# Four tiles for the modulation rows, four fetches ahead, in a two-layer hybrid block

## The chip, the cores and the metric

One core of one Trainium2 chip runs the kernel. The metric is the device time of one execution in microseconds (us); the time before is the median of three runs. The engines are called by their short names: PE (TensorE, matrix products; PEld is its weight load), DVE (VectorE), ACT (ScalarE), POOL (GpSimd) and SP (SyncE, which issues most transfers). DMA engines move data between memory and the core's own SBUF; PSUM takes the products.

## The reference

Two layers, 256 tokens of `x` and 256 of a context `ctx`, width 2048, float32. Each layer begins with a modulation: a vector of 2048 numbers times a matrix of 2048 x 6144, which gives a shift, a scale and a gate. The first layer (even) is a gated delta rule in two directions over 16 heads together with a short convolution; the second (odd) mixes within chunks and pools over rows.

```python
for layer in range(2):
    mod_x = silu(c) @ ada_w[layer] + ada_b[layer]      # 2048 -> 3 * 2048
    sh_x, sc_x, gt_x = split(mod_x, 3)
    h_x = rmsnorm(x, norm_w[layer]) * (1 + sc_x) + sh_x
    # the context likewise, in the first layer only
    if layer == 0:
        y_x, y_c = even_mixer(h_x, h_c, ...)           # delta rule, short convolution, projection out
    else:
        y_x = odd_stream(h_x @ o_w_in, ...)            # chunk mixing, pooling, projection out
    x = x + gt_x * y_x
return rmsnorm(x, final_norm_w)
```

The delta rule needs, per head, direction and chunk of 64 tokens, the inverse of a unit lower triangular matrix, and then a recurrence from chunk to chunk with a state S of 128 x 128.

## The kernel before

**Weights.** All large products run in float32 as three products of a high part H and a remainder L. `wchunk` (L195) fetches a chunk of 128 x 1024 numbers (512 KB) into a tile `raw` (four of them), ACT casts it to H, and DVE or POOL forms L = raw - H; H and L have four tiles each. PE then works through the chunk. The order of the code is not the order of the queues: a planner takes the program and puts each instruction on its engine's queue as soon as, by its own reckoning, the operands and the tile are there, earlier lines first. A transfer that needs a tile stays behind the last reader of the tile's previous content. On the chip every queue then runs strictly in its planned order.

**Stages.** First a projection of the first 1536 key columns with the modulation of the first layer's shift and scale (PE line L449; `h_cols` makes the normalized input and holds a tile `hf` of the modulation rows' pool), then keys and values (`wkv`, PE line L229, with `finish` and the decay rows `ab_rows`), some 180 to 560 us. Then four groups of four heads, some 560 to 1450 us: query and gate projections, the triangular inversion (tiles `Dg`, `LB`, `DT`, and `PTs`, `PTq` in the same places), the recurrence (`St`, `oacc`, `zk`) and the short convolution's projections (`wbb`); inversion and recurrence have high priority. Then the output projection (`wout0`, `projT`, PE lines L238 to L240), the second layer's normalized input `h1`, and from 1600 us on the second layer's projections.

**Modulation rows.** The remaining modulation (the gate of the first layer, all three parts of the second) is not a PE product: 256 steps each fetch a block of 128 x 512 numbers (256 KB) into a tile `araw` (L268) and DVE adds it, times one column of silu(c), to an accumulator `acc` (L274, L276). 16 steps make a segment; `acc` has two tiles. `ada_fin` (L278) sums a segment over the partitions on PE (`adc`), turns it by a second product and adds it to `modc`; the gates go through memory (`rowd`). `ada_step` (L298) is one step in program order: fetch of row u, accumulate of row u - 1, and the end of a segment some steps later. `wchunk` calls it at a rate per chunk, by stage 2.5, 0.6, 1.2 and 0.4; in the third stage no step is taken past the end of the second layer's shift and scale, and ahead of h1 the steps up to there are completed. `araw` has two tiles, in which the constant `mn` and every `hf` also pass.

**What stands beside it.** The first projection has its own tiles `k0`, `k0l` (two each) for H and L. In `ab_rows` the seven decay rows `w` to `br` are tiles of their own.

Of the kernel before, what the change touches and what calls it, by code (L numbers as in the profile page):

```python
# [9 lines left out]
F32 = mybir.dt.float32  # L10
# [7 lines left out]
P = 128  # L18
D = 2048
KT = 16  # L20
# [7 lines left out]
FCUT = (0, 3, 7, 12, 16)  # L28
TAIL = (5, 6)
HP = 1  # L30
FINK = 2
RATE = (2.5, 0.6, 1.2, 0.4)
LP = (0.5, 0.5, 0.4, 0.2)
# [88 lines left out]
def body(ctx: ExitStack, tc: tile.TileContext, T, dbg=None):  # L122
# [21 lines left out]
    whp = pool("wh", NB[1])  # L144
    wlp = pool("wl", NB[2])
# [46 lines left out]
    tick = [0.0, 0.0, 0, 0.0]  # L192

    def wchunk(src, nk, rp=None, hp=None, lp=None, sz=1024, HL=None):
        if extra[0] and hp is None:  # L195
            extra[1] += 1
            rp, hp, lp = extra[0][extra[1] % len(extra[0])]
        raw = (rp or wrawp).tile([P, sz], F32, name="raw", tag="raw")
        dma(raw, src)
        H = HL[0] if HL else (hp or whp).tile([P, sz], F32R, name="H", tag="H")  # L200
        S.copy(H, raw)  # L201
        L = HL[1] if HL else (lp or wlp).tile([P, sz], F32R, name="L", tag="L")
        tick[3] += LP[tick[2]]
        if tick[3] >= 1.0:
            tick[3] -= 1.0
            G.tensor_tensor(L, raw, H, ALU.subtract)  # L206
        else:
            V.tensor_tensor(L, raw, H, ALU.subtract)  # L208
        tick[1] += tick[0]
        while tick[1] >= 1.0:  # L210
            tick[1] -= 1.0
            if tick[2] != 2 or ada_n[0] <= 12 * KT + FINK:
                ada_step()
        return [t.rearrange("p (k c) -> p k c", k=nk) for t in (H, L)]

# [48 lines left out]
    def ada_load(u):  # L264
        w, col = segs[u // 64][:2]
        k, col = u % KT, col + u // KT % 4 * 512
        araw[u] = adap.tile([P, 512], F32, name="araw", tag="araw", bufs=2)
        dma(araw[u], w[k * P:(k + 1) * P, col:col + 512])  # L268

    def ada_acc(u):  # L270
# [22 lines left out]
            S.copy(r, t[0:KT])  # L293
            dma(rowd[gate].rearrange("(a b) -> a b", a=KT), r)

    ADA_N = 256 + 1 + FINK

    def ada_step(n=1):  # L298
        for _ in range(max(0, min(n, ADA_N - ada_n[0]))):
            u = ada_n[0]  # L300
            if u < 256:
                ada_load(u)
            if 1 <= u <= 256:
                ada_acc(u - 1)
            f = u - KT - FINK
            if f >= 0 and f % KT == 0:
                ada_fin(f // KT)
            ada_n[0] += 1
# [55 lines left out]
    with ExitStack() as ph1:  # L364
# [5 lines left out]
        with ExitStack() as ph0:  # L370
# [2 lines left out]
            cs32 = tp.tile([P, KT, 32], F32, name="cs32")  # L373
            V.memset(cs32, 0.0)
            S.copy(cs32[:, :, 0:2], cs)
            k0r, k0p, k0l = pool("k0r", 3, stack=ph0), pool("k0", 2, stack=ph0), pool("k0l", 2, stack=ph0)
            acc = [accp.tile([P, 2, 512], F32, name="kacc", tag=f"kacc{b}") for b in range(6)]

            def ada_cols(j):
# [20 lines left out]
            def load_consts():  # L400
                dma(cst, T["consts"][:, 0:578])
                S.copy(identr, ident)
                t = adap.tile([P, 512], F32, name="mn", tag="araw", bufs=2)[:, 0:256]
                dma(t, T["consts"][:, 578:834])
                S.copy(mneg, t.rearrange("p (a b) -> p a b", a=2))
                S.copy(selr, cst[:, 512:576])
# [22 lines left out]
            def h_cols(j, srcs=(0, 1)):  # L429
                tr = gp.tile([P, 4, P], F32, name="trp", tag="g")  # L430
                for s in srcs:
                    aH, aL = ((hxH, hxL), (hcH, hcL))[s]
                    for n in (2 * s, 2 * s + 1):
                        PE.transpose(tr[:, n, :], toks[n][:, j * P:(j + 1) * P], ident)
                    hf = adap.tile([P, 512], F32, name="hf", tag="araw", bufs=2)[:, 0:256]
                    S.activation(hf, tr[:, 2 * s:2 * s + 2, :].rearrange("p a b -> p (a b)"), AF.Identity,
                                 scale=mods[:, 1, j, s:s + 1], bias=mods[:, 0, j, s:s + 1])
                    split(aH[:, j, :], aL[:, j, :], hf)

            def k_load(e, j):  # L440
                return [t[:, 0] for t in wchunk(T["wset"][e, j], 1, rp=k0r, hp=k0p, lp=k0l, sz=768)]

            def k_part(w, j, ps, first, last, srcs):
                for n in range(6):
# [45 lines left out]
        def row(name):  # L490
            return ap.tile([64, 512], F32, name=name)
# [18 lines left out]
        def ab_rows():  # L510
# [47 lines left out]
                def v4(t):  # L558
                    return t.rearrange("p (c s k) -> p c s k", c=4, s=2)

                w, ng, xr, er, kr, lr, br = (row(n) for n in ("w_", "ng", "xr", "er", "kr", "lr", "br"))
                V.tensor_scalar(ng, gc, -1.0, None, ALU.mult)
                V.tensor_tensor(w.rearrange("p (s k) -> p s k", s=8), glf.unsqueeze(2).to_broadcast([64, 8, 64]),
                                gc.rearrange("p (s k) -> p s k", s=8), ALU.subtract)
# [106 lines left out]
    with ExitStack() as ph2:  # L671
# [6 lines left out]
        for grp in range(4):  # L678
# [48 lines left out]
            with (tc.high_priority() if HP else ExitStack()):  # L727
# [119 lines left out]
                if grp == 0:  # L847
                    tap("U", U.rearrange("p d c h i -> p (d c h i)"))

                St = A.tile([P, 2, 4, P], F32, name="St", tag="St")  # L850
                oacc = [A.tile([P, 4, P], F32, name=f"oacc{c}", tag=f"oacc{c}") for c in range(2)]
                seen = set()
                for s in range(4):
                    for d in range(2):
# [24 lines left out]
                            rh = r[:, h, :] if s > 0 else Vn[:, h, ch, :]  # L879
                            PE.matmul(z[:, h, :], U[:, d, ch, h, :], rh, start=True, stop=True)  # L880
                        if s < 3:
                            zk = A.tile([P, 4, P], F32, name="zk", tag=f"zk{d}")
                            for h in range(4):
                                S.activation(zk[:, h, :], z[:, h, :], AF.Copy, scale=nzs[:, d, ch, h0 + h:h0 + h + 1])
                        if ch < 2:
# [99 lines left out]
    with ExitStack() as ph3:  # L985
# [11 lines left out]
        out_proj(T["wout0"], yact, 0, x1, Wo, pss, (yb_part, [6, 7]), TAIL[0], post0, slots)  # L997
        extra[0] = []
        y_stack.close()
        ada_step(12 * KT + FINK + 1 - ada_n[0])  # L1000
        V.tensor_scalar(A1, mod1[:, KT:2 * KT], 1.0, None, ALU.add)
        V.tensor_tensor(A1, A1, normw[:, KT:2 * KT], ALU.mult)

# [188 lines left out]
```

## Time and profile before

| what | us |
|---|---|
| median of three runs | 2283.49 (2281.34 to 2284.37) |
| the profiled execution's own time | 2281.2 |
| its span | 2279.4 |
| PE busy | 2102.5 (92%) |
| DVE busy | 1511.8 (66%) |
| ACT busy | 992.0 (44%) |
| POOL busy | 547.9 (24%) |
| mean granted clock of PE | 0.968 |

The profile is of one execution. Durations are in us unless marked ns. A wait is the time for which an engine stood idle just before an instruction, put down to what came last; idle time of an engine costs something only where PE comes to stand for it. The granted clock is the share of PE's full clock of 2.4 GHz in a stretch; 0.5 is the lower level of 1.2 GHz.

### The profile page before, as it was taken

How to read it: one execution, taken by the hardware profiler on the slowest of the kernel's cores; microseconds unless marked ns; L12 is line 12 of the kernel's file. 1: busy time of each engine (PE TensorE's matmuls, PEld its weight loads, DVE VectorE, ACT ScalarE, POOL GpSimd, SP SyncE). 2: the span in 40 equal slices, each digit the busy share in tenths (PEclk: the TensorE clock that was granted, in tenths of full speed). 3: DMA queues.
4: the chain of work that ended last, by engine and by line, in shares of the span. 5: the costliest groups of instructions: out<-in, count | busy, mean ns of one | idle time of the engine just before them, and what ended most of it. 6: DMA issues, size and time to landing. Idle time of an engine off the chain costs nothing. (4 is left out here: it accounts for less than half of the span.)

```text
span 2279.4 us, 42114 instructions
## 1 busy us (share of the span) xinstructions
PE 2102.5 (92%) x17034; PEld 1951.4 (86%) x17034; DVE 1511.8 (66%) x2500; ACT 992.0 (44%) x1726; POOL 547.9 (24%) x258
## 2 busy tenths in 40 slices
PE   6998999899989988998899879898999999999998
PEld 4888989898979987998899868686789999999886
DVE  4336997658965896599658964666667676555445
ACT  4332354225544635553545354334444444444443
POOL 0112112123322332323232323232112111111221
PEclk9999999999989999999899989999999999999999
DMA  8776546668435663566356645686767656666664
GB/s 324 278 258 209 153 146 201 192 188 275 141 108 169 213 219 122 170 204 214 120 163 214 205 141 175 200 289 193 251 203 215 180 185 199 188 193 216 192 191 137
DMA packets 151267, 446.41 MB, mean 196 GB/s; under 512 B 16512, under 2 KB 23456, under 8 KB 150048
## 3 DMA queue, kind: packets, MB, share of 16 engines
q1 hardware_dynamic: 145936, 425.37, 58.7%
q0 software_dynamic: 5136, 18.35, 2.6%
q8 instruction: 133, 2.18, 0.4%
q14 instruction: 62, 0.51, 0.1%
HBM read 423.19 MB, written 20.46 MB: 195 GB/s over the span
## 5 line engine op out<-in xcount | busy, mean ns | idle before, releaser
L206 POOL TENSOR_TENSOR L<-raw,H 128x1024 fp32r<-128x1024 f32 (+1 forms) x205 | 508.7, 2483 | 1557.9 <-ACT H L201 1500.2
L201 ACT CAST H<-raw 128x1024 fp32r<-128x1024 f32 (+1 forms) x554 | 571.9, 1039 | 698.7 <-PE pj L229 302.3
L208 DVE TENSOR_TENSOR L<-raw,H 128x1024 fp32r<-128x1024 f32 (+1 forms) x349 | 447.8, 1285 | 311.2 <-ACT H L201 310.1
L229 PE MATMUL pj<-hxH,L 128*128 128x256 f32 x1856 | 537.7, 290 | 43.9 <-DVE L L208 43.7
L229 PE MATMUL pj<-hxH,H 128*128 128x256 f32 x1856 | 536.1, 289 | 4.8 <-DVE kacc L482 4.8
L229 PE MATMUL pj<-hxL,H 128*128 128x256 f32 x1856 | 535.0, 288 | 0.0
L229 PEld LDWEIGHTS pj<-hxH,L 128*128 128x128 f32 x1856 | 360.2, 194 | 51.6 <-DVE L L208 48.1
L229 PEld LDWEIGHTS pj<-hxH,H 128*128 128x128 f32 x1856 | 360.2, 194 | 6.9 <-DVE kacc L482 5.0
L229 PEld LDWEIGHTS pj<-hxL,H 128*128 128x128 f32 x1856 | 360.3, 194 | 1.4 <-issue 0.4
L276 DVE SCALAR_TENSOR_TENSOR acc<-araw,cs,acc 128x512 f32<-128x512 f32 x240 | 244.9, 1020 | 134.3 <-DMA araw<-in_ada 84.0
L229 PE MATMUL pj<-h1H,H 128*128 128x256 f32 x1024 | 290.6, 284 | 0.8 <-DVE yo L1052 0.8
L229 PE MATMUL pj<-h1H,L 128*128 128x256 f32 x1024 | 289.8, 283 | 0.0
L229 PE MATMUL pj<-h1L,H 128*128 128x256 f32 x1024 | 289.8, 283 | 0.0
L229 PEld LDWEIGHTS pj<-h1H,H 128*128 128x128 f32 x1024 | 196.5, 192 | 1.1 <-PE adc L286 0.8
L229 PEld LDWEIGHTS pj<-h1L,H 128*128 128x128 f32 x1024 | 196.5, 192 | 0.0
L229 PEld LDWEIGHTS pj<-h1H,L 128*128 128x128 f32 x1024 | 196.5, 192 | 0.0
L229 PE MATMUL pj<-hcH,H 128*128 128x256 f32 x320 | 92.0, 287 | 0.0
L229 PE MATMUL pj<-hcH,L 128*128 128x256 f32 x320 | 91.6, 286 | 0.0
L229 PE MATMUL pj<-hcL,H 128*128 128x256 f32 x320 | 91.5, 286 | 0.0
L238 PE MATMUL pj<-H,y1H 128*128 128x512 f32 x192 | 76.0, 396 | 0.0
L240 PE MATMUL pj<-H,y1L 128*128 128x512 f32 x192 | 75.9, 396 | 0.0
L239 PE MATMUL pj<-L,y1H 128*128 128x512 f32 x192 | 75.9, 395 | 0.0
(433 smaller groups left out, 3852.3 us busy)
## 6 DMA issues: line engine op xcount, KB each, us to landing
raw<-in_wbb SPq DMA_DIRECT2D x128, 512.0 KB, 4.1
raw<-in_wout SPq DMA_DIRECT2D x128, 512.0 KB, 4.5
araw<-in_ada SPq DMA_DIRECT2D x192, 256.0 KB, 3.4
raw<-in_ada SPq DMA_DIRECT2D x64, 512.0 KB, 6.4
raw<-in_wpz SPq DMA_DIRECT2D x64, 512.0 KB, 4.1
raw<-in_wuz SPq DMA_DIRECT2D x64, 512.0 KB, 3.9
raw<-in_wkv SPq DMA_DIRECT2D x40, 512.0 KB, 4.7
araw<-in_ada0g SPq DMA_DIRECT2D x64, 256.0 KB, 3.6
```

Of the source, the lines that this page charges most:

```text
L201: S.copy(H, raw)
L206: G.tensor_tensor(L, raw, H, ALU.subtract)
L208: V.tensor_tensor(L, raw, H, ALU.subtract)
L229: PE.matmul(o[:, e * 256:(e + 1) * 256] if m > 1 else o, w, a[t][:, k, :], start=st and i == 0 and e == 0, stop=sp and i == 2, skip_group_ ...
L238: PE.matmul(o, xH[:, t], H[:, kk, :], start=st, stop=False, skip_group_check=True)
L239: PE.matmul(o, xH[:, t], L[:, kk, :], start=False, stop=False, skip_group_check=True)
L240: PE.matmul(o, xL[:, t], H[:, kk, :], start=False, stop=sp, skip_group_check=True)
L276: V.scalar_tensor_tensor(aacc[u // KT], raw, cs[:, k, 0:1], aacc[u // KT], ALU.mult, ALU.add)
```

## The change

`araw` gets four tiles, and a row's accumulate stands four steps behind its fetch instead of one. The number of steps grows from 259 to 262, the end of a segment comes three steps later, and the two guards that count steps grow alike. Three further things change: the first projection uses the common H and L tiles (four each) instead of its own; two rows of `ab_rows` reuse the tiles of `y` and `q`; and `St`, `oacc` (both chunks in one tile) and `zk` (both directions in one tile) of the recurrence pass through the tiles `LB`, `DT` and `Dg` of the inversion.

```diff
--- before.py
+++ after.py
@@ -28,6 +28,7 @@
 FCUT = (0, 3, 7, 12, 16)
 TAIL = (5, 6)
 HP = 1
+LA = 4
 FINK = 2
 RATE = (2.5, 0.6, 1.2, 0.4)
 LP = (0.5, 0.5, 0.4, 0.2)
@@ -209,7 +210,7 @@
         tick[1] += tick[0]
         while tick[1] >= 1.0:
             tick[1] -= 1.0
-            if tick[2] != 2 or ada_n[0] <= 12 * KT + FINK:
+            if tick[2] != 2 or ada_n[0] < 12 * KT + FINK + LA:
                 ada_step()
         return [t.rearrange("p (k c) -> p k c", k=nk) for t in (H, L)]
 
@@ -264,7 +265,7 @@
     def ada_load(u):
         w, col = segs[u // 64][:2]
         k, col = u % KT, col + u // KT % 4 * 512
-        araw[u] = adap.tile([P, 512], F32, name="araw", tag="araw", bufs=2)
+        araw[u] = adap.tile([P, 512], F32, name="araw", tag="araw", bufs=LA)
         dma(araw[u], w[k * P:(k + 1) * P, col:col + 512])
 
     def ada_acc(u):
@@ -293,16 +294,16 @@
             S.copy(r, t[0:KT])
             dma(rowd[gate].rearrange("(a b) -> a b", a=KT), r)
 
-    ADA_N = 256 + 1 + FINK
+    ADA_N = 256 + LA + FINK
 
     def ada_step(n=1):
         for _ in range(max(0, min(n, ADA_N - ada_n[0]))):
             u = ada_n[0]
             if u < 256:
                 ada_load(u)
-            if 1 <= u <= 256:
-                ada_acc(u - 1)
-            f = u - KT - FINK
+            if LA <= u < 256 + LA:
+                ada_acc(u - LA)
+            f = u - KT - FINK - LA + 1
             if f >= 0 and f % KT == 0:
                 ada_fin(f // KT)
             ada_n[0] += 1
@@ -373,7 +374,7 @@
             cs32 = tp.tile([P, KT, 32], F32, name="cs32")
             V.memset(cs32, 0.0)
             S.copy(cs32[:, :, 0:2], cs)
-            k0r, k0p, k0l = pool("k0r", 3, stack=ph0), pool("k0", 2, stack=ph0), pool("k0l", 2, stack=ph0)
+            k0r = pool("k0r", 3, stack=ph0)
             acc = [accp.tile([P, 2, 512], F32, name="kacc", tag=f"kacc{b}") for b in range(6)]
 
             def ada_cols(j):
@@ -400,7 +401,7 @@
             def load_consts():
                 dma(cst, T["consts"][:, 0:578])
                 S.copy(identr, ident)
-                t = adap.tile([P, 512], F32, name="mn", tag="araw", bufs=2)[:, 0:256]
+                t = adap.tile([P, 512], F32, name="mn", tag="araw", bufs=LA)[:, 0:256]
                 dma(t, T["consts"][:, 578:834])
                 S.copy(mneg, t.rearrange("p (a b) -> p a b", a=2))
                 S.copy(selr, cst[:, 512:576])
@@ -432,13 +433,13 @@
                     aH, aL = ((hxH, hxL), (hcH, hcL))[s]
                     for n in (2 * s, 2 * s + 1):
                         PE.transpose(tr[:, n, :], toks[n][:, j * P:(j + 1) * P], ident)
-                    hf = adap.tile([P, 512], F32, name="hf", tag="araw", bufs=2)[:, 0:256]
+                    hf = adap.tile([P, 512], F32, name="hf", tag="araw", bufs=LA)[:, 0:256]
                     S.activation(hf, tr[:, 2 * s:2 * s + 2, :].rearrange("p a b -> p (a b)"), AF.Identity,
                                  scale=mods[:, 1, j, s:s + 1], bias=mods[:, 0, j, s:s + 1])
                     split(aH[:, j, :], aL[:, j, :], hf)
 
             def k_load(e, j):
-                return [t[:, 0] for t in wchunk(T["wset"][e, j], 1, rp=k0r, hp=k0p, lp=k0l, sz=768)]
+                return [t[:, 0] for t in wchunk(T["wset"][e, j], 1, rp=k0r, hp=whp, lp=wlp, sz=768)]
 
             def k_part(w, j, ps, first, last, srcs):
                 for n in range(6):
@@ -558,7 +559,7 @@
                 def v4(t):
                     return t.rearrange("p (c s k) -> p c s k", c=4, s=2)
 
-                w, ng, xr, er, kr, lr, br = (row(n) for n in ("w_", "ng", "xr", "er", "kr", "lr", "br"))
+                w, ng, xr, er, kr, lr, br = (row(n) for n in ("w_", "ng", "xr", "er", "kr", "y_", "q_"))
                 V.tensor_scalar(ng, gc, -1.0, None, ALU.mult)
                 V.tensor_tensor(w.rearrange("p (s k) -> p s k", s=8), glf.unsqueeze(2).to_broadcast([64, 8, 64]),
                                 gc.rearrange("p (s k) -> p s k", s=8), ALU.subtract)
@@ -847,8 +848,10 @@
                 if grp == 0:
                     tap("U", U.rearrange("p d c h i -> p (d c h i)"))
 
-                St = A.tile([P, 2, 4, P], F32, name="St", tag="St")
-                oacc = [A.tile([P, 4, P], F32, name=f"oacc{c}", tag=f"oacc{c}") for c in range(2)]
+                St = I.tile([P, 2, 4, P], F32, name="St", tag="LB")
+                oac2 = I.tile([P, 2, 4, P], F32, name="oacc", tag="DT")
+                oacc = [oac2[:, c] for c in range(2)]
+                zk2 = I.tile([P, 2, 4, P], F32, name="zk", tag="Dg")
                 seen = set()
                 for s in range(4):
                     for d in range(2):
@@ -879,7 +882,7 @@
                             rh = r[:, h, :] if s > 0 else Vn[:, h, ch, :]
                             PE.matmul(z[:, h, :], U[:, d, ch, h, :], rh, start=True, stop=True)
                         if s < 3:
-                            zk = A.tile([P, 4, P], F32, name="zk", tag=f"zk{d}")
+                            zk = zk2[:, d]
                             for h in range(4):
                                 S.activation(zk[:, h, :], z[:, h, :], AF.Copy, scale=nzs[:, d, ch, h0 + h:h0 + h + 1])
                         if ch < 2:
@@ -997,7 +1000,7 @@
         out_proj(T["wout0"], yact, 0, x1, Wo, pss, (yb_part, [6, 7]), TAIL[0], post0, slots)
         extra[0] = []
         y_stack.close()
-        ada_step(12 * KT + FINK + 1 - ada_n[0])
+        ada_step(12 * KT + FINK + LA - ada_n[0])
         V.tensor_scalar(A1, mod1[:, KT:2 * KT], 1.0, None, ALU.add)
         V.tensor_tensor(A1, A1, normw[:, KT:2 * KT], ALU.mult)
```

## Rows read from the trace of the kernel before

**Rows 1.** The page's first part: the span, and busy time, share and number of instructions of each engine.

```profile
span 2279.4 us, 42114 instructions
PE 2102.5 (92%) x17034; PEld 1951.4 (86%) x17034; DVE 1511.8 (66%) x2500; ACT 992.0 (44%) x1726; POOL 547.9 (24%) x258
```

**Rows 2.** The view of waits for PE alone (who waited, for whom: us in total, times, longest us), in four stretches one after the other: 182 to 560 us (three rows), 570 to 1310 us (one), 570 to 660 us (one), 1456 to 1674 us (four).

```profile
PE kvp L598 <- DVE kvT L362: 20.8, 10, 4.6
PE pj L229 <- DVE kacc L482: 4.8, 1, 4.8
PE adr L291 <- DVE modc L288: 1.8, 1, 1.8
...
PE pj L229 <- DVE L L208: 43.7, 20, 7.4
...
PE pj L229 <- DVE L L208: 11.3, 5, 5.9
...
PE pj L239 <- DVE L L208: 10.1, 6, 4.4
PE pg L239 <- DVE L L208: 3.2, 2, 2.2
PE pg L238 <- ACT H L201: 2.9, 1, 2.9
...
PE pj L240 <- DVE h1L L345: 1.5, 1, 1.5
```

**Rows 3.** The page's fifth part, groups of instructions: line, engine, operation, out<-in, shape, count | busy us, mean ns of one | idle time of the engine before them, and what ended most of it.

```profile
L206 POOL TENSOR_TENSOR L<-raw,H 128x1024 fp32r<-128x1024 f32 (+1 forms) x205 | 508.7, 2483 | 1557.9 <-ACT H L201 1500.2
L201 ACT CAST H<-raw 128x1024 fp32r<-128x1024 f32 (+1 forms) x554 | 571.9, 1039 | 698.7 <-PE pj L229 302.3
...
L276 DVE SCALAR_TENSOR_TENSOR acc<-araw,cs,acc 128x512 f32<-128x512 f32 x240 | 244.9, 1020 | 134.3 <-DMA araw<-in_ada 84.0 <-DMA araw<-in_ada0g 48.6
```

**Rows 4.** The view of the tile araw, its last line: time from a fetch's issue to its landing, least, median and most, of the whole run and then of the stretch from 505 to 545 us.

```profile
DMA to landing us min/median/max: 2.5/3.5/7.8
...
DMA to landing us min/median/max: 2.9/5.3/7.8
```

**Rows 5.** The view of waits for DVE alone, its rows on the modulation rows, in three stretches: 182 to 560 us (two rows), 570 to 1310 us, 1456 to 1674 us.

```profile
DVE acc L276 <- DMA araw<-in_ada0g: 48.6, 31, 3.3
DVE acc L276 <- DMA araw<-in_ada: 20.7, 16, 3.0
...
DVE acc L276 <- DMA araw<-in_ada: 15.7, 19, 1.9
...
DVE acc L276 <- DMA araw<-in_ada: 47.6, 32, 3.8
```

**Rows 6.** The timeline of DVE, about 224 and about 1668 us: start us, length us, what, in brackets the idle time before it and what ended that.

```profile
224.04 0.75 DVE L276 SCALAR_TENSOR_TENSOR acc<-araw,cs,acc 128x512 f32<-128x512 f32 x1 [3.12 <-DMA araw<-in_ada0g]
...
225.21 1.22 DVE L482 TENSOR_TENSOR kacc<-kacc,pj 128x1024 f32<-128x1024 f32 x1
...
1668.11 0.75 DVE L276 SCALAR_TENSOR_TENSOR acc<-araw,cs,acc 128x512 f32<-128x512 f32 x1 [3.71 <-DMA araw<-in_ada]
1668.78 5.64 DVE L208 TENSOR_TENSOR L<-raw,H 128x1024 fp32r<-128x1024 f32 x3
```

**Rows 7.** The timeline of PE at the same two places.

```profile
226.48 0.58 PE L229 MATMUL pj<-hxH,H 128*128 128x256 f32 x1 [4.75 <-DVE kacc L482]
...
1672.21 0.80 PE L239 MATMUL pj<-L,h1H 128*128 128x512 f32 x1 [4.42 <-DVE L L208]
```

**Rows 8.** Busy time of each engine in three stretches of 7 us that begin where PE resumes; after POOL stand the granted clock of PE, the busy share of the DMA engines and GB/s.

```profile
224.00:231.00 7.00, 4.52 (x21) 4.52 (x22) 5.14 (x6) 2.28 (x3) 0.00 (x0) 0.54 0.53 164
436.00:443.00 7.00, 5.25 (x25) 5.29 (x26) 6.66 (x11) 1.58 (x3) 0.00 (x0) 0.51 0.59 176
1549.00:1556.00 7.00, 4.28 (x10) 3.06 (x11) 4.12 (x4) 1.19 (x2) 0.64 (x1) 0.52 0.67 209
```

**Rows 9.** The view of waits for SP's queue (L268 issues the modulation rows) from 1456 to 1674 us.

```profile
SPq L268 <- DVE acc L276: 51.1, 52, 2.5
```

**Rows 10.** The views of the tiles adc (the end of a segment; its second product) and gts (the gate in the residual addition, from 2000 us on): count, duration ns least/median/most, first and last start us, shape.

```profile
L286 PE MATMUL adc<-cst,ads x32: 167/252/376, 367.6 to 2026.1; 128*128 128x4 f32 x32
...
L657 DVE TENSOR_TENSOR opt<-pj,gts x6: 684/688/692, 2134.1 to 2224.3; 128x512 f32<-128x512 f32 x6
```

**Rows 11.** The views of the tiles PTs, St and Dg, each in a stretch that holds one group (the first for PTs and St, the second for Dg); columns as in the group before.

```profile
L818 PE MATMUL X<-U,PTs x128: 191/191/212, 659.8 to 661.0; 32*32 32x32 f32 x128
...
L868 PE MATMUL QS<-St,QT x32: 275/275/275, 700.0 to 732.3; 128*128 128x128 f32 x32
...
L893 ACT COPY St<-Sp x2: 586/604/623, 677.6 to 682.2; 128x512 f32<-128x512 f32 x2
...
L768 ACT COPY Dg<-U x4: 1137/1142/1153, 794.2 to 801.7; 32x512 f32<-32x512 f32 x4
```

**Rows 12.** Busy time of each engine in four stretches: PE, PEld, DVE, ACT, POOL, each with its number of instructions, then the granted clock, the busy share of the DMA engines and GB/s.

```profile
0.00:57.00 57.00, 37.85 (x330) 27.85 (x330) 24.82 (x70) 28.35 (x50) 5.29 (x7) 0.94 0.89 324
...
1456.00:1554.00 98.00, 89.85 (x377) 70.84 (x370) 67.17 (x68) 34.71 (x44) 31.11 (x13) 0.95 0.81 263
1588.00:1669.00 81.00, 73.21 (x333) 57.72 (x325) 53.31 (x64) 33.48 (x47) 14.82 (x11) 1.00 0.78 247
...
1482.00:1539.00 57.00, 57.00 (x246) 45.88 (x245) 39.42 (x35) 20.09 (x23) 20.58 (x8) 1.00 0.85 287
```

## The prediction

> **What bounds the kernel now.** I read the page's first part before anything else: PE is busy for 2102.5 of 2279.4 us [rows 1], so the time is PE's work plus the 176.9 us in which it stands still. What the change can be worth lies in those gaps, so the next view is who PE waited for. It is nearly always VectorE (DVE), by stage [rows 2]: 27.4 us in the first stage (20.8 + 4.8 + 1.8 of its rows), 43.7 us for the weight remainders L in the recurrence's stage, and 17.7 us in the output stage (10.1 + 3.2 + 2.9 + 1.5).
>
> Then I ask why DVE is late. The modulation accumulates cost DVE 1.02 us each and 244.9 us in all, and it stood idle for 134.3 us in front of them, waiting for their rows to land [rows 3]. By stage those waits are 48.6 + 20.7 us in the first, 15.7 us in the recurrence's and 47.6 us in the output stage [rows 5]. DVE runs its queue in order, so whatever stands behind such an accumulate waits with it. Two places show it whole. At 224.04 an accumulate starts after 3.12 us of waiting, the addition into kacc runs behind it at 225.21, and PE starts at 226.48 after 4.75 us of standing. At 1668.11 the wait was 3.71 us, three L follow at 1668.78, and PE starts at 1672.21 after 4.42 us [rows 6, 7].
>
> A stop costs PE more than itself. After three of the linked stops the granted clock is 0.54, 0.51 and 0.52 over 7 us [rows 8], that is, mostly the lower of its two levels; that loses 7 x 0.46, 7 x 0.49 and 7 x 0.48, together 10.0 us.
>
> **The change, part by part.**
>
> Four tiles, four fetches ahead. No accumulate, fetch or matmul is added or removed; what changes is the distance. With two tiles the fetch of a row can go when the accumulate two before it is done, so one other accumulate and whatever lies between must cover a landing of 3.5 us [rows 4]. With four tiles three accumulates cover it: 2 x 1.02 = 2.04 us more of DVE's own work. The waits that occur are far shorter than that on average (in the output stage 47.6 us in 32 waits, 1.5 us each), and the longest is 3.8 us [rows 5]. Taken alone this would cover most of them. Against it stands that landings grow when more is moving: in the stretch from 505 to 545 us the median is 5.3 us [rows 4], 1.8 us over the whole run's, and that eats most of the 2.04. The bounds are therefore nothing and all of it: 0 to 27.4 + 17.7 + 10.0 = 55.1 us. I take half, 27.5 us, because neither row is nearer: the cover that is added and the growth of the landing are about equal, and the rows of a burst still come in the order in which the queues were planned. What is late next, where a stall goes, is the L or the addition itself, at DVE's own speed.
>
> The recurrence's stage I cost at nothing, between a loss of 6 and a gain of 10 us. PE lost 11.3 us there between 570 and 660 us [rows 2], a stretch with no accumulate in it, so most of the stage's 43.7 us is DVE's own work. The gain is what part of the 15.7 us of waits can reach PE; the loss is two more accumulates that have landed and go ahead of the inversion, 2.04 us in each of three bursts.
>
> The fetches on SP. SP stood for 51.1 us in the output stage at fetches that waited for an accumulate [rows 9], with weight loads queued behind them. The fetch now waits for an accumulate two further back, so this wait shrinks with the others. It is the same gain seen from SP and is not counted again. In exchange up to 1 MB of rows instead of 0.5 MB can be in the air beside the weights. One stop of PE in the output stage already came from a cast that was late, 2.9 us [rows 2]. I charge one more such stop, 2.9 us; the bound above it is the third rival.
>
> The end of each segment comes three steps later, since the accumulates trail the fetches by four. The last of them ran at 2026.1 us; three steps are 7.5 weight chunks at 0.4 steps a chunk, some 21 us, and the first product that needs its row stands at 2134.1 [rows 10]. It is covered by 87 us and costs nothing. The others are moved within slack of the same kind, and no step is moved past the guard ahead of h1, because the guard grows with LA.
>
> St, zk and oacc in the inversion's tiles. This adds waits: the first copy into St on ACT must wait for the readers of PTs, and the next group's inversion for the last readers of zk and St; behind the first stand ACT's other copies of the recurrence, behind the second the whole next inversion on ACT and DVE. Neither comes late: the last matmul that reads PTs starts at 661.0 and St is first written at 677.6; the last product with St starts at 732.3 and the next Dg is first written at 794.2 [rows 11]. It costs nothing while 16 and 61 us of cover stand; if they were gone, the wait would be as long as the lateness, and no row comes near that.
>
> The first projection takes its weight tiles from the common pool of four instead of its own two, and two rows of the decay reuse others that DVE itself has finished with. The second has one answer, nothing. The first gives that phase two tiles more and takes from the phase behind it four that stood free; if the boundary were bare, one cast and one remainder would show, 1.04 + 2.48 us [rows 3]. The gain is bounded by the same 3.5 us. I take nothing.
>
> Sum against the profiled execution's own 2281.2 us (its span and 1.8 us around it): 2281.2 - 27.5 + 2.9 = 2256.6. The median of the runs is 2.3 us above that execution, so 2259.
>
> **The rivals.**
>
> All of it. The waits vanish and PE's linked stops with their low clocks go, 55.1 us. For it: the mean wait of 1.5 us is below the 2.04 us of new cover. Against it: landings of 5.3 us where traffic is dense. It gives 2283.5 - 55.1 = 2228.
>
> Nothing. DVE's idle time shrinks, but PE's stops are set by the chains that end in kvT or in L, whose work is unchanged; the accumulates merely come earlier and the same additions wait for their own inputs. For it: the recurrence's stage, which stalls without any accumulate. Against it: the two places in [rows 6, 7], where the wait for a row stands directly in front of what PE waited for. It gives 2283.
>
> Slower, by crowding in the output stage. A weight chunk of 524,288 bytes feeds 12 matmuls, and 246 of them take 57 us, so the weights need 189 GB/s [rows 12]. The two bursts of 32 rows there now last 98 and 81 us, 3.1 and 2.5 us a row. If the waits went entirely, a row could come every (3.5 + 1.02) / 4 = 1.13 us, which is 232 GB/s more: 421 in all, against 324, the highest rate of a stretch in the trace [rows 12]. The excess of 97 GB/s over 36 us is 3.5 MB, or 10.8 us at 324 GB/s, in each burst; with a low clock of 3.4 us behind each it is 28.4 us. It decides when rows come faster than one in 1.94 us, where the sum passes 324 GB/s. With half the first stage's gain, (27.4 + 6.6) / 2 = 17.0, it gives 2283.5 + 28.4 - 17.0 = 2295. For it: the share of DMA is already 0.81 and 0.78 in these bursts, and a late cast has stopped PE there. Against it: weights are loaded several chunks ahead. The Trainium skill, Perfetto Trace Analysis, section Roofline, puts the practical ceiling of a single core at the some 435 GB/s of its 16 DMA engines; by that 421 GB/s would still pass, this rival's price would be zero, and the sum would be the forecast's or better. No stretch of this trace moves more than 324 GB/s, so it is not shown here.
>
> That the change doesn't do what it says: the fetch of a row is written ahead of the accumulate that frees its tile, so it can leave only after that one, and the planner may leave three rows in the air where four are meant. That would cost a quarter of the gain, 7 us, and lies inside the forecast's range.
>
> **How the numbers follow.** Forecast 2259, chance 0.52; all of it, 2228, 0.16; nothing, 2283, 0.13; crowding, 2295, 0.19. 0.2% is about what a measurement of this kernel can tell from no change, so faster means under 2279 and slower over 2288. Faster is the first two, 0.68; same 0.13; slower 0.19. The range runs from the full gain, 2230, to the edge of the slower side, 2288; it leaves out a part of the first and most of the last rival.
>
> **What would show it.** Right: DVE's idle time in front of the accumulates falls from 134 to below 70 us, bursts in the first and the output stage get shorter, the stops at 221 and 1668 us are gone with the low clock behind them, and PE's work stays at 2102 us less what the clock gave back. Wrong: the bursts are shorter but casts wait longer for weights (crowding); the waits are gone and PE stops as before for L or kvT (nothing); or accumulates packed in a row stand in front of the inversion and PE stops longer between 750 and 1310 us, which no term above prices beyond 6 us.

## The result, and the profile after

The changed kernel takes 2231.53 us (median of 4 runs, 2229.27 to 2233.19) against 2283.93 us of the kernel before beside it: 0.9776 of its time, 95% interval 0.9757 to 0.9796, or 52 us less. The forecast was 2259. The direction was right and 2231.5 lies in the range, but the gain is twice the 24.6 us forecast. The time is close to that of the rival "all of it", 2228, by luck: the experiments put some 40 us down to the row tiles, not 55, and some 13 to the shared tiles.

The page's first part and one group of its fifth part (busy us, mean ns of one | idle time before, what ended most of it), of the kernel after:

```profile
span 2231.4 us, 42172 instructions
PE 2091.3 (94%) x17034; PEld 1946.6 (87%) x17034; DVE 1521.7 (68%) x2500; ACT 995.0 (45%) x1726; POOL 548.3 (25%) x258
...
L277 DVE SCALAR_TENSOR_TENSOR acc<-araw,cs,acc 128x512 f32<-128x512 f32 x240 | 242.8, 1012 | 42.1 <-DMA araw<-in_ada 24.2
```

PE stands still for 2231.4 - 2091.3 = 140.1 us where it was 176.9 [rows 1], and its own work is shorter by 2102.5 - 2091.3 = 11.2 us, with the same 17034 matmuls: 36.8 + 11.2 are the 48.0 us between the spans. DVE's idle time in front of the accumulates fell from 134.3 [rows 3] to 42.1 us.

Where PE's 36.8 us came from is read by stage. The view of windows (length, then busy time of PE, PEld, DVE, ACT and POOL, each with its count, then the granted clock, the DMA share and GB/s) in three stages: up to the first matmul into rq, from there to the last one into oT, and from there to the first one into sp. First of before:

```profile
0.00:549.60 549.60, 499.87 (x4268) 465.01 (x4269) 352.75 (x645) 207.18 (x410) 103.44 (x51) 0.98 0.68 223
549.60:1455.40 905.80, 813.45 (x7735) 776.23 (x7738) 667.06 (x1202) 440.50 (x864) 268.69 (x114) 0.95 0.55 173
1455.40:1736.40 281.00, 258.62 (x1336) 215.57 (x1336) 194.38 (x256) 117.74 (x168) 71.97 (x39) 0.97 0.73 234
```

And of after, with the two bursts of the output stage as the last two lines:

```profile
0.00:537.80 537.80, 493.60 (x4254) 459.36 (x4255) 359.79 (x652) 206.38 (x412) 101.67 (x50) 0.98 0.69 230
537.80:1397.80 860.00, 781.91 (x7595) 752.05 (x7595) 642.34 (x1169) 427.48 (x847) 254.97 (x110) 0.95 0.53 168
1397.80:1686.30 288.50, 283.30 (x1483) 239.07 (x1483) 221.13 (x283) 133.99 (x184) 87.32 (x42) 1.00 0.80 266
1551.00:1610.00 59.00, 59.00 (x269) 48.76 (x262) 48.52 (x61) 26.89 (x37) 12.29 (x10) 1.00 0.88 293
1399.00:1508.00 109.00, 109.00 (x474) 87.53 (x475) 93.55 (x91) 44.94 (x55) 43.35 (x16) 0.99 0.92 314
```

Length less PE's busy time is PE's idle time: 49.7 to 44.2 us in the first stage, 92.4 to 78.1 in the recurrence's, 22.4 to 5.2 in the output stage (the stages' lengths don't compare, because matmuls moved from one to the next). In both bursts PE is busy from end to end: in the later one (1551 to 1610 us) at a granted clock of 1.00 with 293 GB/s moving, in the earlier one at 0.99 with 314. The output stage now holds 48 + 32 rows where it held 64; 16 moved into it from the recurrence's.

The waits of PE alone in the kernel after, in the stretches of 182 to 560 us, 560 to 1310 us and 1440 to 1674 us (us in total, times, longest):

```profile
PE kvp L599 <- DVE kvT L363: 11.9, 6, 4.1
PE kvp L599 <- DVE gc L540: 6.8, 1, 6.8
PE kvp L599 <- DVE nrs L615: 2.3, 1, 2.3
PE pj L450 <- DVE kacc L483: 1.6, 1, 1.6
...
PE pj L230 <- DVE L L209: 32.4, 15, 5.1
PE PT L807 <- DVE UT L798: 15.5, 4, 5.3
...
PE pj L239 <- ACT h1H L345: 2.5, 1, 2.5
PE pj L240 <- DVE L L209: 2.4, 1, 2.4
```

Against [rows 2], kvT fell from 20.8 to 11.9 us, the stop of 4.8 us for kacc at 226 us is gone (the 1.6 us left is at another line, L450, which had 1.2 us before), L in the recurrence's stage fell from 43.7 to 32.4 (but the inversion's UT rose from 10.3 to 15.5), and the output stage from 17.7 to 4.9 us. In the first stage new names stand where the old ones were (gc, nrs), and its four rows still add up to 22.6 us. The waits of DVE in the same three stretches:

```profile
DVE acc L277 <- DMA araw<-in_ada0g: 15.3, 14, 3.1
...
DVE acc L277 <- DMA araw<-in_ada: 7.5, 7, 1.9
...
DVE acc L277 <- DMA araw<-in_ada: 1.7, 2, 1.1
...
DVE acc L277 <- DMA araw<-in_ada: 14.7, 11, 2.4
```

The 32 waits of 47.6 us of the output stage [rows 5] are 11 of 14.7 us. The last lines of the view of araw (issue to landing, of the run, of 1399 to 1508 and of 1551 to 1610 us) show that the price was paid that the prediction feared, and that it did not matter:

```profile
DMA to landing us min/median/max: 2.5/4.4/9.3
...
DMA to landing us min/median/max: 2.9/5.3/7.3
...
DMA to landing us min/median/max: 2.8/5.6/8.6
```

One stop of the old kind is left, where the last burst ends. Timeline of DVE, kernel after (start, length, in brackets the idle time before), and then of PE:

```profile
1599.33 0.75 DVE L277 SCALAR_TENSOR_TENSOR acc<-araw,cs,acc 128x512 f32<-128x512 f32 x1
1599.99 1.22 DVE L209 TENSOR_TENSOR L<-raw,H 128x1024 fp32r<-128x1024 f32 x1
1601.13 1.53 DVE L277 SCALAR_TENSOR_TENSOR acc<-araw,cs,acc 128x512 f32<-128x512 f32 x2
1602.58 1.22 DVE L209 TENSOR_TENSOR L<-raw,H 128x1024 fp32r<-128x1024 f32 x1
...
1608.90 0.75 DVE L277 SCALAR_TENSOR_TENSOR acc<-araw,cs,acc 128x512 f32<-128x512 f32 x1 [2.42 <-DMA araw<-in_ada]
1609.56 5.67 DVE L209 TENSOR_TENSOR L<-raw,H 128x1024 fp32r<-128x1024 f32 x3
```

```profile
1613.02 0.50 PE L240 MATMUL pj<-L,h1H 128*128 128x512 f32 x1 [2.37 <-DVE L L209]
```

It is the figure of [rows 6, 7] at 1668 us again, a wait, three L behind it, and PE; but 2.42 and 2.37 us where it was 3.71 and 4.42, and no low clock follows (1.00 from 1613 to 1620 us, where the kernel before had 0.50 from 1672 to 1675).

### The profile page after: what moved, and what is told of

It is laid out like the page before. It is cut to its first block, busy times and chain, and to the rows that moved or that the text cites. A ratio compares the mean times of both kernels' runs of the same rounds, so it can differ in the third digit from the quotient of the medians.

```text
span 2231.4 us, 42172 instructions
## 1 busy us (share of the span) xinstructions
PE 2091.3 (94%) x17034; PEld 1946.6 (87%) x17034; DVE 1521.7 (68%) x2500; ACT 995.0 (45%) x1726; POOL 548.3 (25%) x258
## 5 line engine op out<-in xcount | busy, mean ns | idle before, releaser
L230 PE MATMUL pj<-hxH,L 128*128 128x256 f32 x1856 | 538.1, 290 | 32.5 <-DVE L L209 32.4
L277 DVE SCALAR_TENSOR_TENSOR acc<-araw,cs,acc 128x512 f32<-128x512 f32 x240 | 242.8, 1012 | 42.1 <-DMA araw<-in_ada 24.2
```

The costliest lines, as they stand in the source:

```text
L230: PE.matmul(o[:, e * 256:(e + 1) * 256] if m > 1 else o, w, a[t][:, k, :], start=st and i == 0 and e == 0, stop=sp and i == 2, skip_group_ ...
L277: V.scalar_tensor_tensor(aacc[u // KT], raw, cs[:, k, 0:1], aacc[u // KT], ALU.mult, ALU.add)
```

## The experiments

Medians in us beside the kernel before in the same job, ratio with its 95% interval; DVE's waits for rows are the two lines of the view of araw added up; PE's idle time is length less busy time in the three stages above (the fourth, 12.2 to 13.1 us everywhere, is left out). e7 and e8 leave work out.

| run | row tiles | shared tiles | time | ratio | DVE waits | PE idle: first, recurrence, output |
|---|---|---|---|---|---|---|
| before | 2 | none | 2283.9 | 1 | 136 | 49.7, 92.4, 22.4 |
| after | 4 | all | 2231.5 | 0.9776 (0.9757 to 0.9796) | 42 | 44.2, 78.1, 5.2 |
| e1 | 2 | all | 2271.8 | 0.9944 (0.9927 to 0.9962) | 136 | 57.6, 87.0, 14.9 |
| e2 | 4, written one ahead | all | 2234.1 | 0.9775 (0.9756 to 0.9794) | 46 | 45.0, 83.2, 4.3 |
| e3 | 4 from row 192 on | all | 2267.0 | 0.9914 (0.9895 to 0.9933) | 114 | 54.8, 88.5, 9.0 |
| e4 | 4 up to row 192 | all | 2255.1 | 0.9864 (0.9847 to 0.9882) | 85 | 43.8, 78.3, 19.3 |
| e5 | 2 | first projection | 2282.7 | 0.998 (0.9962 to 0.9998) | 133 | 51.3, 94.7, 17.9 |
| e6 | 2 | St, oacc, zk | 2276.5 | 0.9952 (0.9932 to 0.9971) | 133 | 47.4, 92.3, 17.0 |
| e7 | no fetch | all | 2228.2 | 0.9738 (0.971 to 0.9766) | 0 | 34.6, 78.5, 12.7 |
| e8 | 4, thin work | all | 2222.3 | 0.9715 (0.9688 to 0.9741) | 114 | 46.0, 68.9, 10.9 |
| e9 | 2, FINK 3 | none | 2291.8 | 1.0045 (1.0028 to 1.0061) | 143 | 55.7, 92.9, 22.7 |
| e10 | 3 | all | 2246.0 | 0.9843 (0.9821 to 0.9866) | 75 | 46.8, 80.1, 4.4 |
| e11 | 4, FINK 0 | all | 2240.0 | 0.9818 (0.9795 to 0.9841) | 41 | 45.8, 84.1, 3.5 |
| e12 | 4, more L on POOL | all | 2243.9 | 0.9834 (0.9812 to 0.9856) | 48 | 46.7, 84.0, 4.9 |
| e13 | 4, FINK 1 | all | 2240.2 | 0.981 (0.9792 to 0.9828) | 49 | 46.1, 83.4, 4.5 |
| e14 | 4, FINK 3 | all | 2230.5 | 0.9766 (0.9749 to 0.9782) | 37 | 39.4, 86.7, 3.8 |
| e15 | 4 | without oacc, zk | 2233.6 | 0.9776 (0.9755 to 0.9797) | 46 | 44.0, 75.7, 8.5 |

**Which half of the change does it: e1, e2.** Kernel after with two row tiles, and with four tiles but the program written one fetch ahead.

```diff
-LA = 4
+LA = 1
-        araw[u] = adap.tile(..., tag="araw", bufs=LA)
+        araw[u] = adap.tile(..., tag="araw", bufs=2)      # e1; 4 in e2
```

> Two tiles for the modulation rows and one fetch ahead as before; the shared tiles of the first projection, of the decay rows and of St, oacc and zk as after. Theory (the four row tiles alone carry the gain, by covering landings): 2284 us, within 6 us of before. Rival (the shared tiles, or the planner's new order that they bring, carry the 12 us by which the recurrence's stage got shorter, or more): 2272 us or less.

> Four row tiles, but the accumulate written one step behind its fetch, as before. Theory (what counts is how many rows can be in the air, since the planner moves fetches ahead as far as the tiles allow): 2232 us, within 8 us of the changed kernel. Rival (the distance written in the program counts): half the gain or less, 2258 us or more.

e1 hits its rival: with two row tiles the rest of the change brings 12.8 us. e2 hits the theory: what counts is the number of tiles, and the distance that is written in the program makes no difference that can be measured. So the two further tiles are worth 2271.8 - 2231.5 = 40.3 us (by the two ratios 38, with some 6 us of uncertainty from their intervals).

**In which stage: e3, e4.** Kernel after; odd rows from 192 on (e3), or below 192 (e4), take two tiles of their own, the others share two (with `mn` and `hf`).

```diff
-        araw[u] = adap.tile(..., tag="araw", bufs=LA)
+        araw[u] = adap.tile(..., tag="arow2" if u >= 192 and u % 2 else "araw", bufs=2)
```

> Four row tiles only for the rows from 192 on (the output stage), two for the rows ahead of them; all else as after. Theory (the output stage gains its whole 23 us of stops and low clock there, the first stage some 10): 2260 us. Rival (the 12 us of the recurrence's stage come from what the output stage can take over): 2248 us.

> Four row tiles only for rows 0 to 191 (first stage and recurrence), two for the rows from 192 on. Theory: first stage 8 to 12 us and recurrence 12 us remain gained, the output stage stands as before: 2260 us. Rival (the gain of the output stage comes from the early rows' order): 2240 us or less.

Each moves PE's idle time where its rows are: e4 takes the first stage from 57.6 to 43.8 us and leaves the output stage (19.3), e3 takes the output stage from 14.9 to 9.0 and leaves the first (54.8). In time they bring 16.7 and 4.8 us beyond e1, 21.5 together, where both at once bring 40.3; the stages don't add up. e4 came out near its theory, e3 above both of its numbers. In both, `hf` has two tiles as before, and e4's first stage still stands as the kernel after's (44.2): the gain there is the rows' and not hf's.

**Which of the shared tiles: e5, e6.** Kernel before with the first projection's weight tiles from the common pool alone, and with St, oacc and zk in the inversion's tiles alone (hunks of the diff, nothing else).

> The kernel before, and of the change only the first projection's use of the common H and L tiles. If one of the shared tiles is the cause of the 13 us that the shared tiles gained together, it is here or in the next run: 2271 us in one and 2284 us in the other. Rival (there is no single cause; any change of the tiles gives the planner another order, and each order falls some us to one side or the other): both within 8 us of before, and neither the whole 13.

> The kernel before, and of the change only St, oacc and zk in the inversion's tiles. A cause here would show in the recurrence's stage, whose stops and low clock were 12 us less with all shared tiles: 2272 us. Rival (planner's order): within 8 us of before, the difference spread over stages that the tiles don't touch.

They bring 3.3 and 9.5 us, together what e1 has; the 9.5 lies between the theory's 13 and the rival's 8. No single wait of PE carries it: the output stage lost 4.5 and 5.4 us of idle time, a stage in which neither edit touches a tile.

**What is left of the waits: e7.** Kernel after; the accumulates read a constant tile, and the modulation rows are not fetched (256 rows of 262,144 bytes are left out, and the modulation is not that of the reference).

```diff
-        araw[u] = adap.tile([P, 512], F32, name="araw", tag="araw", bufs=LA)
-        dma(araw[u], w[k * P:(k + 1) * P, col:col + 512])
+        araw[u] = cst[:, 0:512]
```

> The changed kernel without the fetches of the modulation rows: every accumulate reads a constant tile, so the products of the modulation are left out, and with them 64 MB of traffic and all waits for landings; DVE's work is the same. Theory (with four tiles the waits that remain, 42 us on DVE, hardly reach PE, and the traffic of the bursts costs next to nothing): 2226 us, 2216 to 2236. Rival (crowding takes back part of the gain): 2212 us or less, the output stage's waits of casts for weights gone.

No row is waited for, no row is moved, and the time is 3.4 us lower than after's by the medians (8.7 by the ratios). That is a net. In the first stage PE stands for 34.6 us instead of 44.2, in the output stage for 12.7 instead of 5.2. Waits of PE in e7, from 182 to 560 us and from 1400 to 1740:

```profile
PE kvp L598 <- DVE kvT L362: 5.3, 3, 2.8
PE kvp L598 <- DVE gc L539: 2.7, 1, 2.7
...
PE pj L240 <- POOL L L207: 4.9, 4, 2.5
```

In the first stage the 22.6 us of waits in the kernel after are 8.0, so the rows that are still late there seem to cost PE some 10 us; in the output stage PE comes to wait for POOL's L. In all, the 42 us that DVE still waits and 64 MB of extra traffic together cost no more than some 9 us, and the output stage stands no less without that traffic: the crowding rival has no room left.

**What the accumulates' own work costs: e8.** Kernel after; each accumulate works on 32 of its 512 columns (the rest of the modulation is left out), fetches as they are.

```diff
-            V.scalar_tensor_tensor(aacc[u // KT], raw, ...)
+            V.scalar_tensor_tensor(aacc[u // KT][:, 0:32], raw[:, 0:32], ...)
```

> The changed kernel with accumulates of 32 columns instead of 512 (all but the first row of a segment; the rest of the products is left out), fetches and waits as they are: DVE has some 200 us less to do. Theory (what is left of PE's stops in the first stage and the recurrence, some 160 us with their low clock, is DVE's own work, the accumulates among it): 2200 us or less. Rival (the stops hang on chains that don't pass through the accumulates): 2222 us or more.

The theory fell and the rival's bound is just met. The page's first part and the group of the accumulates, in e8:

```profile
PE 2083.1 (94%) x17034; PEld 1938.0 (87%) x17034; DVE 1389.5 (63%) x2500; ACT 994.1 (45%) x1726; POOL 537.3 (24%) x258
...
L277 DVE SCALAR_TENSOR_TENSOR acc<-araw,cs,acc 128x32 f32<-128x32 f32 x240 | 107.8, 450 | 111.0 <-DMA araw<-in_ada 71.2
```

DVE has 132 us less to do than in the kernel after, but the accumulates now wait 111.0 us for their rows instead of 42.1: about half of what DVE saved it waited again, and PE's idle time only went from 140.1 to 2221.2 - 2083.1 = 138.1 us. The 9.3 us by which e8 is faster than the kernel after are mostly PE's own work, 8.2 us less.

**Order alone: e9, e11, e13, e14.** FINK, the number of steps from a segment's last accumulate to its end, changed in the kernel before (e9) and in the kernel after (the others).

```diff
-FINK = 2
+FINK = 3        # e9, e14; 0 in e11, 1 in e13
```

> The kernel before with the end of each modulation segment written one step later (FINK 3 instead of 2): no work, no tile and no transfer changes, only the order that the planner makes. Theory (a new order alone moves this kernel by some us either way, which is what the shared tiles did): at least 4 us away from before, 2276 to 2291 us, on either side. Rival (the order alone is worth nothing, so the 13 us of the shared tiles have a cause in the tiles): 2284 us, within 3 us of before.

> The changed kernel with the end of each segment two steps earlier (FINK 0), so that the accumulates of group 2 of the recurrence may run there again (32 instead of 19) instead of in the output stage. Theory (accumulates in the recurrence's stage cost PE little, as the narrow accumulates showed): 2232 us, within 6 us of the changed kernel. Rival (their place makes the recurrence's gain): 2240 us or more.

> The kernel after with FINK 1 in place of 2: the end of each segment is taken in one step earlier, everything else as it is, four tiles and shared tiles included. Only the order of the work changes. The kernel after has 0.978 of the time of before (2231.5 us), FINK 0 gave 2240. Theory (the 13 us that the shared tiles brought are of the size of what any change of the order does): the runs with FINK 0, 1, 2 and 3 do not lie in a line and spread over 6 us or more, with this one anywhere from 2228 to 2245. Rival (an earlier segment end costs time step by step): this one lies between 2233 and 2238, and FINK 3 at 2231 or below.

> The kernel after with FINK 3 in place of 2: the end of each segment one step later. Theory (order alone moves the time by several us either way): at least 4 us from the 2231.5 of the kernel after, or out of line with FINK 0 and 1. Rival (the later the end of a segment, the better, by some 4 us a step from FINK 0's 2240): 2227 to 2231.

FINK 3 costs the kernel before 9 us and the kernel after nothing. In the kernel after, FINK 0, 1, 2 and 3 give 2240.0, 2240.2, 2231.5 and 2230.5: a step between 1 and 2 (7.8 us by the ratios, with some 6 of uncertainty), not the 4 us a step of the rival (whose bound e11 and e14 meet, and e13 does not). The spread of 9.7 us is what the theory said, but e14 is neither 4 us off nor out of line, so the theory's own condition for it is met only in part. What it does give is a size: moving an end by one step, with no tile and no work changed, moves the time by up to 9 us, and not to the same side in both kernels.

One stop that comes and goes with the order can be named. PE begins the output projection with the short convolution's part (tiles ybH and ybL), and in the kernel before DVE makes ybL at 1326.2 us, right behind an inversion. Waits of PE from 1150 to 1450 us in before, e1, e11 and after:

```profile
PE pj L240 <- DVE ybL L345: 9.6, 1, 9.6
...
PE pj L241 <- DVE ybL L346: 8.7, 1, 8.7
...
PE pj L241 <- DVE ybL L346: 8.9, 1, 8.9
...
PE pj L241 <- DVE ybL L346: 0.7, 1, 0.7
```

With ybH's waits added it is 10.7 us in before, 10.4 in e1, 10.5 in e11, 6.8 in e13 and 10.4 in e2, but 4.2 in e5, 0.7 in after, 2.1 in e14, 1.1 in e15 and 0.6 in e3. It doesn't go by the tiles (e2 has four; e3 has two for the rows ahead of it). It is as long as what FINK makes in the kernel after, and as the recurrence's gain from e1 to after, but it isn't shown to be the cause: e2 has the whole stop and is no slower than the kernel after.

**The third tile, POOL's share, two tiles given back: e10, e12, e15.** Kernel after with LA = 3 and three tiles (e10); with the second entry of LP at 0.6 instead of 0.5, so that POOL makes more of the L (e12); and with oacc and zk in tiles of their own again (e15).

> The changed kernel with three row tiles and three fetches ahead. Theory (each tile adds one accumulate of 1.02 us of cover; the mean wait of 1.35 us is covered by the third tile for the most part): two thirds of the 40 us that four tiles gain over two, 2245 us, DVE's waits for rows 80 us or less. Rival (the landing grows as fast as the cover): 2258 us or more.

> The changed kernel with 0.6 instead of 0.5 of the weight remainders of the recurrence's stage on POOL (2.48 us each there, 1.28 us on DVE). Theory (what stops PE there is DVE's own queue, 32 us of waits for L): some 20 remainders less on DVE, 25 us of its work, 2225 us. Rival (POOL's slower remainder becomes what PE waits for): 2235 us or more.

> The kernel after with oacc and zk back in tiles of their own; St stays in the tile LB, the first projection stays in the common pool, four row tiles. Rival (sharing the recurrence's tiles itself brought the 9.5 us of the run that had it alone, oacc and zk among it): giving two of the three back costs 4 us or more, 2236 or above. Theory (it came from the order that the sharing happened to make, not from the tiles): the time moves by a few us to either side with no tie to the tiles, 2225 to 2235.

Three tiles bring 25.8 of the 40.3 us, two thirds, as the theory had it. e12 is 12 us slower, as its rival had it in time, though not by its mechanism. Waits of PE from 560 to 1310 us in e12:

```profile
PE PT L807 <- DVE UT L798: 22.8, 5, 7.3
PE pj L230 <- DVE L L209: 21.5, 8, 5.5
PE E L747 <- DVE aT L759: 11.5, 7, 2.6
```

The L fell from 32.4 to 21.5 us as meant, and no row names POOL; PE waits longer for the inversion's steps on DVE instead (UT 15.5 to 22.8, aT 3.3 to 11.5). Twelve us are little more than what order alone moves, so this reading is argued and not shown. e15 changes nothing that can be measured.

## Why the prediction was half right

**What bounds the kernel: right.** PE's time is its work and its stops, and the stops in the first and the output stage came in good part from rows that had not landed while DVE's queue stood. From e1 to the kernel after only the row tiles and the distance change (and the queues' order with them): DVE's waits go from 136 to 42 us, and 40.3 us of time go with them. The rival "nothing" is refuted by the same pair. The rival that three rows would be in the air where four are meant falls by the trace: in the kernel after a row's fetch leaves, in the median, 0.03 us after the end of the accumulate four rows back.

**"I take half, 27.5 us": the step that failed.** It was to be 27.5 less 2.9 for crowding, 24.6 us; it measured 40.3. Its reason was that "the cover that is added and the growth of the landing are about equal", 2 x 1.02 = 2.04 us against 1.8. The traces give both sizes. The landing's median grew by 0.9 us over the whole run (3.5 to 4.4), and in the output stage's two bursts from 4.1 to 5.3 and from 3.6 to 5.6, so 1.8 is about right for the bursts and twice too much for the run. The cover was too small. Taken row by row, the time from the end of the accumulate that frees a tile to DVE's arrival at the accumulate that uses it next has a median of 3.97 us in before, 4.31 in e1, 5.60 in e10 and 7.13 in after: two more tiles added some 3 us, not 2.04. What passes there is not only the other accumulates but all that DVE does among them: the timeline at 1599 us has an L of 1.22 us after every one or two accumulates. The bursts of before took 3.1 and 2.5 us a row, as the prediction itself worked out, and 2.4 and 1.7 without DVE's waits in them (22.1 and 27.4 us), so the larger size could be had from its own rows. e10's theory counted 1.02 us a tile and came out too; the time of that run can't tell 1.0 from 1.3.

Split with e1 as the start, the 40.2 us between the two spans (2271.6 and 2231.4) are 13.4 us of PE's idle time in the first stage, 8.9 in the recurrence's, 9.7 in the output stage, and 8.5 us of PE's own work (2099.8 to 2091.3). This split is not firm by stage. Against before the same lines are 5.5, 14.3, 17.2 and 11.2 us, and e14, with four tiles, has 86.7 us of idle time in the recurrence's stage, no less than e1. What holds over all the runs is this: the first and the recurrence's stage together stand for 139.7 to 148.6 us in the six runs with two tiles for their rows and for 119.7 to 130.7 in the eight full ones with four, and the output stage for 14.9 to 22.7 and for 3.5 to 9.0. By the means that is 18 us of the 27.4 and 10 that the prediction gave these two stages at most, and 13.6 of the output stage's 17.7. So the recurrence's stage, costed at nothing, may well have given a part, but no run sets it apart from the first, and the stop for ybL alone is worth its 8.9 us.

The clock's term was itself too large. Two of the stretches of [rows 8] begin before PE resumes (224 and 436 us; it resumes at 226.48 and 437.7). From there the granted clock over 7 us is 0.65 and 0.62, and 0.66 from 1551 to 1558: that loses 7.5 us and not 10.0. PE's work fell by 8.5 us from e1 to after, and by 11.2 from before.

**"I charge one more such stop, 2.9 us": wrong.** No cast was late: PE is busy for 109.00 of 109.00 and 59.00 of 59.00 us in the bursts, at 314 and 293 GB/s. The rival "crowding" was to decide at 1.94 us a row; the last burst ran at 1.8, and e7 shows that the rows' traffic and the waits for it together cost no more than some 9 us. What was wrong in it was the rate: it put a row every 1.13 us, 421 GB/s in all, where DVE's pace with its L between never asked for more than these. The Trainium skill, Perfetto Trace Analysis, section Roofline, has the practical ceiling of a single core at some 435 GB/s; no run here moves enough to test it. The highest slice of the profile's page is 342 GB/s in the kernel after, and 358 in e12, above the 324 that the rival took as the limit.

**The shared tiles, "It costs nothing" and "I take nothing": right in their reasons, 12.8 us off in the sum.** No wait for a shared tile shows up, and the covers held: in the first group the last reader of PTs starts at 642.8 us and St is first written at 660.8, and the last product with St starts at 713.9 and the next Dg at 781.1. But every such edit moves the queues' order, and e1, e5 and e6 gained 12.8, 3.3 and 9.5 us. That is the size of what FINK alone does (9 us). e15 gives back two of the shared tiles with no loss. It speaks against the tiles oacc and zk as the cause and for the order; it doesn't show it, since the order of the kernel before was not kept while the tiles were changed, and St stays shared in e15. Which step of the order brought e6 its 9.5 us stays open, as does why FINK 0 and 1 cost the kernel after 8.5 us. Together the two misses, 40.3 - 24.6 = 15.7 and 12.8, are the 28 us between forecast and time.

**The ends of segments three steps later, the decay rows, SP: right.** No wait on an end or on SP shows in PE's rows of the output stage, and the later ends of FINK 2 and 3 are the better ones.

**The signs given.** DVE's waits below 70 us (42), shorter bursts and PE's work less what the clock gave back (11.2 of 10.0) came as said; the stop at 221 us is gone (no wait of PE from 205 to 260 us, granted clock 1.00 from 224 to 231), and the one at the end of the last burst is halved and has lost its low clock, but is not gone.

## What to carry to other kernels

Where an in-order engine stands for a transfer, the cover of a further tile is what the engine does per transfer in all (here some 1.4 us in the median from one tile count to the next), not the duration of the instruction that consumes it (1.02 us). If the mean wait is below that, as here with 1.5 us against two further tiles, start from the full gain and look for a reason to take less; here 40 of 55 us came. How many tiles there are counts, not how far ahead the program is written. Any edit that moves a tile or a step under a planned order can move this kernel by the order alone, FINK by up to some 0.45%; this belongs in the range, and an effect of that size is not put down to the edit without a second order to compare with.

## What was not expected of the hardware

An accumulate's 1.01 us is a mean of two things. In the kernel after, 65 of the 256 accumulates share some of their time with an instruction on POOL and take 1.74 us in the mean (27 of them no longer than alone); the other 191 take 0.73, and not one of them over 1.0. It shows best in e8, where the work is a sixteenth. Timeline of DVE, then of POOL, in e8:

```profile
216.14 0.25 DVE L277 SCALAR_TENSOR_TENSOR acc<-araw,cs,acc 128x32 f32<-128x32 f32 x1
...
218.23 2.46 DVE L277 SCALAR_TENSOR_TENSOR acc<-araw,cs,acc 128x32 f32<-128x32 f32 x1
```

```profile
218.03 2.61 POOL L207 TENSOR_TENSOR L<-raw,H 128x1024 fp32r<-128x1024 f32 x1 [9.77 <-ACT H L202]
```

The same instruction takes 0.25 us alone and 2.46 us beside a POOL L, and ends at 220.69, when that L ends (220.64). The Trainium skill, SBUF — State Buffer, section Who interferes with whom, has a VectorE instruction with two SBUF inputs contend with a GpSimd instruction that reads SBUF; the trace agrees. Some 65 x 1.0 us of DVE's time in the kernel after is such standing, none of it marked as a wait. No run took POOL's L away, so what it costs the kernel is not shown.
